# Two transformer-like blocks on one core: the first block's dense products made 512 wide, its gates moved to transposed heads, its differential heads put into fixed TensorE steps

## The chip, the cores and the metric

The kernel runs on one core of one Trainium2 chip. It computes two different blocks one after the other for a sequence of 512 positions and a model width of 1024, in float32 accuracy. The metric is the device time of the whole kernel in microseconds (us); lower is better. The engines are named as in the profile: PE (TensorE, matmul), PEld (its weight loads), DVE (VectorE), ACT (ScalarE), POOL (GpSimd), SP (SyncE, which issues the DMAs).

## The reference

The change is in the first block alone. Cut to what matters, it is:

```python
h = rms_norm(x, norm_g)                                # x: 512 x 1024
z = h @ w_in                                           # 9216 columns, split into ten parts:
q_r, k_r, v_r, gate_r, q_d, k_d, v_d, gate_d, mg_r, mg_d = split(z)
o_r = rms_norm(retention(q_r, k_r, v_r))               # 8 heads, 4 chunks of 128, state carried from chunk to chunk
y_r = (o_r * silu(gate_r)) @ ret_w_o
qd, kd = rms_norm(q_d), rms_norm(k_d)                  # 8 heads, two 64-wide halves each
p = softmax(qd kd^T - slope * dist)                    # causal, one for each half
o_d = rms_norm((p[0] - lam * p[1]) @ v_d)              # differential attention
y_d = (o_d * silu(gate_d)) @ diff_w_o
m = sigmoid(mg_r) * y_r + sigmoid(mg_d) * y_d
x = x + m @ w_out
```

The second block (`..._2`) is another attention layer on that `x`; it is about a third of the span, and its code stays as it is but for the names of some buffers.

## The kernel before

**Products.** Every dense product is made of three matmuls on split operands (`mm3`, L314 to L317): each float32 operand is held as a rounded `hi` and a remainder `lo`, and `hi*hi + hi*lo + lo*hi` is summed in PSUM. Weights come through a `Streamer` in a fixed order (`st.add`, `st.get`): a part of 512 KB is loaded by SP into `wr` (2 buffers), ACT rounds it to `wh` (L128), DVE subtracts to `wl` (L130); `wh` and `wl` have 4 buffers each.

**Two forms of dense product.** `dense_T` has 128 weight columns stationary and all 512 positions moving: its output is transposed (columns on partitions), 512 wide. `dense_TM` has 128 positions stationary and a weight of 256 columns moving: its output has positions on partitions, two tiles of 256 columns share a PSUM tile, and all of one position tile's eight k steps come before the next tile's. `v_r`, `g_r`, `q_d`, `k_d`, `v_d`, `g_d` go through `dense_TM` (tile `dps`), four weights of 256 columns each; `q_r`, `k_r` (`rps`), `mg_*` and `y_*` (`mps`) go through `dense_T`. The output projection `wo` is a `dense_TM` of its own (tile `ops` with `mh`, `ml`).

**Heads.** A pair of retention heads is one chain over four chunks (`rsp`, `rop`, `stp`, `sbd`). A differential head has four steps t of 128 queries: two pairs of score matmuls (`sp`), DVE adds the table `tb` and takes the minimum (L479), ACT exponentiates (L483), DVE joins the two halves (L671 to L673), PE transposes (`apt`), ACT copies (`aT`), PE multiplies with the values (`dop`); at the end the row norm (POOL, L259 and L260), `gated` (L454) multiplies with norm and gate, and `to_oT` transposes (`ogp`) and splits the result.

**Order.** Up to the last weight of `wo` no order of PE is written down: a planner with simulated times takes from the program, instruction by instruction, what it thinks is ready, earlier lines first, and fixes each engine's order when the kernel is built. The program's own order is: retention by groups with its gates, `q_d0 k_d0 v_d0 g_d0`, `mg_r` and `y_r`, then head pair by head pair the attention and the next pair's dense products, `mg_d`, `y_d`, `wo`. From `wo3` on, through the second block, PE runs in the program's order (`tc.manual_schedule`), where one attention step, a share of dense work (`fill`), and the transposes and products of earlier steps follow each other. PSUM: `ps_d` 3 buffers (dense), `ps_t` 2, `ps_s` 2, `ps_o` 1.

Of the kernel before, what the change touches and what calls it, by code (L numbers as in the profile page):

```python
# [32 lines left out]
T_AT = [(0, 2), (0, 5), (1, 0), (1, 2), (1, 4), (1, 6)]  # L33
# [10 lines left out]
QK_BUFS = 12  # L44
LAM0 = 0.8 - 0.6 * math.exp(-0.0)
# [101 lines left out]
def two_block_kernel(ctx: ExitStack, tc: tile.TileContext, A: dict, out: bass.AP):  # L147
# [31 lines left out]
    for g in range(2):  # L179
        for hp in (2 * g, 2 * g + 1):  # L180
            add_k8(f"v_r{hp}", w_in, 1024 + 256 * hp)
            add_k8(f"g_r{hp}", w_in, 2048 + 256 * hp)
            if hp == 2 * g:
                add_k8(f"q_r{g}", w_in, 256 * g)
                add_k8(f"k_r{g}", w_in, 512 + 256 * g)

    def add_diff(hp):
        for nm, base in (("q_d", 3072), ("k_d", 4096), ("v_d", 5120), ("g_d", 6144)):
            add_k8(f"{nm}{hp}", w_in, base + 256 * hp)

    add_diff(0)
    for g in range(4):
        add_k8(f"mg_r{g}", w_in, 7168 + 256 * g)
        add_k8(f"y_r{g}", ret_w_o, 256 * g)
    for hp in range(1, 4):
        add_diff(hp)
    for g in range(4):
        add_k8(f"mg_d{g}", w_in, 8192 + 256 * g)
    for g in range(4):
        add_k8(f"y_d{g}", diff_w_o, 256 * g)  # L200
    for g in range(4):
        add_k8(f"wo{g}", w_out, 256 * g)
# [44 lines left out]

    def spread_row(row, pool):
        ones = pool.tile([1, P], F32, name="ones")
        nc.vector.memset(ones, 1.0)  # L250
        full = pool.tile([P, D], F32, name="full")
        for i in range(2):
            ps = ps_s.tile([P, S], F32, name="rowp", tag="s")
            nc.tensor.matmul(ps, ones, row[:, S * i : S * i + S], start=True, stop=True)
            nc.scalar.activation(full[:, S * i : S * i + S], ps, AF.Copy)
        return full
# [62 lines left out]
    def dense_T(tiles, n0, act_hi, act_lo, name):  # L319
        ps = ps_d.tile([P, S], F32, name=name, tag="d")  # L320
        for kt in range(KT):
            hi, lo = tiles[kt // 4]
            k4 = kt % 4
            mm3(ps, hi[:, k4, n0 : n0 + P], lo[:, k4, n0 : n0 + P],
                act_hi[kt], act_lo[kt], kt == 0, kt == KT - 1)
        return ps

    def dense_TM(tiles, tp, act_hi, act_lo, name, n=256):
        ps = ps_d.tile([P, 2, n], F32, name=name, tag="d")
        for i in range(2):  # L330
# [54 lines left out]
    oT_pool = ctx.enter_context(tc.tile_pool(name="oT", bufs=8))  # L385
# [6 lines left out]
    def new_oT(name):  # L392
        hi = oT_pool.tile([P, S], F32R, name=name + "h", tag="oh")
        lo = oT_pool.tile([P, S], F32R, name=name + "l", tag="ol")
        return hi, lo
# [56 lines left out]
    def gated(o4, scal, w4, og4):  # L452
        for i in range(4):
            nc.vector.scalar_tensor_tensor(og4[:, i, :], o4[:, i, :], scal[:, i : i + 1], w4[:, i, :],  # L454
                                           op0=ALU.mult, op1=ALU.mult)

    def to_oT(og, h, col, name):
        pt = ps_t.tile([P, NT, P], F32, name="ogp", tag="t")
        for t in range(NT):
            nc.tensor.transpose(pt[:, t, :], og[:, t, h * P : (h + 1) * P], ident)  # L460
# [730 lines left out]
```

## Time and profile before

| | us |
|---|---|
| three runs | 972.47, 975.05, 977.28; median 975.05 |
| the profiled execution, its own time | 973.76 |
| its span from first to last instruction | 971.7 |
| mean granted TensorE clock | 0.982 of full |

The profile page gives busy time by engine, the span in slices, and the chain of work that ended last. Matmul ends are modelled and matmuls overlap, so the summed or mean time of a matmul is longer than the distance from one start to the next; that distance, the pace, is what a stream of matmuls costs. Windows are stretches of the span in us.

### The profile page before, as it was taken

Reading aid. Unit: us, or ns where it says so; the run is one execution under the profiler, and the core shown is the slowest. Engines: PE = TensorE matmul, PEld = TensorE weight load, DVE = VectorE, ACT = ScalarE, POOL = GpSimd, SP = SyncE. Lnnn points to the kernel's source line nnn. Section 1 sums busy time; section 2 is a strip of 40 time slices with the busy share of each in tenths; the row PEclk is TensorE's granted clock in tenths of the full one; section 3 lists DMA queues with packets and bytes.
Section 4 is the critical chain, followed back from the end, with each engine's and each line's share of the span. In section 5 each row is a group of like instructions: output and inputs, shape, how many; then the busy total and the mean of one; then the engine's idle time right before and its main releaser. Section 6 shows DMA issues by size and latency. Waiting matters only on the chain.

```text
span 971.7 us, 16383 instructions
## 1 busy us (share of the span) xinstructions
PE 940.3 (97%) x6457; PEld 858.0 (88%) x6457; DVE 556.3 (57%) x1255; ACT 439.3 (45%) x917; POOL 208.7 (21%) x242
## 2 busy tenths in 40 slices
PE   7899999999999999999997988999999899999998
PEld 6889989999888999999996876899998778999886
DVE  4544434463332647647655465535556897778884
ACT  5323222343222545555644453233446666666650
POOL 2000001032000016115113100034146563332000
PEclk9999999999999999999998998999999899999999
DMA  6451232135343322212221212544242231211412
GB/s 202 135 170 45 87 109 87 48 118 165 109 131 129 96 79 87 73 60 88 70 77 59 85 48 65 171 136 153 67 136 70 57 97 44 66 44 45 142 55 87
DMA packets 78047, 92.18 MB, mean 95 GB/s; under 512 B 5081, under 2 KB 66409, under 8 KB 77971
## 3 DMA queue, kind: packets, MB, share of 16 engines
q1 hardware_dynamic: 77970, 91.14, 29.9%
q8 instruction: 51, 0.84, 0.3%
q14 instruction: 26, 0.21, 0.1%
HBM read 84.82 MB, written 8.93 MB: 96 GB/s over the span
## 4 chain that ended last, share of the span: by engine, by line
PE 88%; DVE 6%; DMA 2%; ACT 1%; issue 1%; SPq 1%; POOL 1%; ACTq 0%; POOLq 0%; DVEq 0%
PE dps L315 9%; PE dps L317 9%; PE dps L316 9%; PE mps L315 6%; PE mps L316 6%; PE mps L317 6%; PE ops L315 3%; PE ops L316 3%; PE ops L317 3%; PE aps L315 2%; PE aps L316 2%; PE aps L317 2%; PE dop L681 2%; PE rps L315 1%; PE rps L317 1%; PE rps L316 1%
## 5 line engine op out<-in xcount | busy, mean ns | idle before, releaser
L316 PE MATMUL dps<-wl,h1h 128*128 128x256 f32 x768 | 221.2, 288 | 3.4 <-DVE wl L130 3.4
L315 PE MATMUL dps<-wh,h1h 128*128 128x256 f32 x768 | 222.6, 290 | 1.3 <-ACT h1h L277 1.3
L317 PE MATMUL dps<-wh,h1l 128*128 128x256 f32 x768 | 221.6, 289 | 0.2 <-DVE h1l L278 0.2
L130 DVE TENSOR_TENSOR wl<-wr,wh 128x1024 fp32r<-128x1024 f32 (+2 forms) x115 | 141.4, 1231 | 127.6 <-ACT wh L128 124.9
L128 ACT ACTIVATE wh<-wr 128x1024 fp32r<-128x1024 f32 (+1 forms) x132 | 137.4, 1042 | 166.6 <-PE mps L316 60.0
L316 PEld LDWEIGHTS dps<-wl,h1h 128*128 128x128 f32 x768 | 147.6, 192 | 4.2 <-DVE wl L130 3.8
L315 PEld LDWEIGHTS dps<-wh,h1h 128*128 128x128 f32 x768 | 147.6, 192 | 3.6 <-ACT h1h L277 1.8
L317 PEld LDWEIGHTS dps<-wh,h1l 128*128 128x128 f32 x768 | 147.5, 192 | 1.4 <-issue 0.5
L315 PE MATMUL aps<-wh,h2h 128*128 128x256 f32 x192 | 57.0, 297 | 0.0
L316 PE MATMUL aps<-wl,h2h 128*128 128x256 f32 x192 | 54.3, 283 | 0.0
L317 PE MATMUL aps<-wh,h2l 128*128 128x256 f32 x192 | 54.3, 283 | 0.0
L663 POOL TENSOR_SCALAR tb<-dist 128x512 f32<-128x512 f32 x8 | 13.7, 1712 | 186.2 <-DVE nm L479 156.6
L315 PE MATMUL mps<-h1h,wh 128*128 128x512 f32 x128 | 51.3, 401 | 0.9 <-ACT td L721 0.9
L317 PE MATMUL mps<-h1h,wl 128*128 128x512 f32 x128 | 51.1, 399 | 0.0
L316 PE MATMUL mps<-h1l,wh 128*128 128x512 f32 x128 | 50.8, 397 | 0.0
L483 ACT ACTIVATE p<-sc,nm 128x128 f32<-128x128 f32 (+3 forms) x64 | 35.7, 559 | 33.0 <-DVE nm L479 29.4
L130 POOL TENSOR_TENSOR wl<-wr,wh 128x1024 fp32r<-128x1024 f32 (+2 forms) x17 | 38.1, 2242 | 40.9 <-ACT wh L128 31.6
L1009 ACT ACTIVATE p<-p,nm 128x128 f32<-128x128 f32 (+1 forms) x64 | 35.7, 558 | 20.3 <-DVE nm L1006 19.9
L479 DVE CUSTOM_DVE_ANT_0 sc<-sp,tb 128x128 f32<-128x128 f32 (+3 forms) x64 | 30.3, 488 | 25.4 <-PE sp L312 25.0
L260 POOL TENSOR_TENSOR gnrs<-gnrs,mhalf 128x8 f32<-128x8 f32 x24 | 40.4, 1687 | 1.8
L316 PEld LDWEIGHTS aps<-wl,h2h 128*128 128x128 f32 x192 | 36.7, 191 | 0.3
L317 PE MATMUL ops<-wh,ml 128*128 128x256 f32 x128 | 36.9, 290 | 0.0
(297 smaller groups left out, 2379.5 us busy)
## 6 DMA issues: line engine op xcount, KB each, us to landing
wr<-in_w_in_dram SPq DMA_DIRECT2D x92, 512.0 KB, 3.6
wr<-in_w_out_dram SPq DMA_DIRECT2D x16, 512.0 KB, 3.5
wr<-in_ret_w_o_dram SPq DMA_DIRECT2D x8, 512.0 KB, 3.6
wr<-in_diff_w_o_dram SPq DMA_DIRECT2D x8, 512.0 KB, 3.2
rep_dram<-rev_dram SPq DMA_DIRECT2D x8, 320.0 KB, 8.8
m_dram<-mth SPq DMA_DIRECT2D x8, 256.0 KB, 2.5
mr<-m_dram SPq DMA_DIRECT2D x8, 256.0 KB
x<-in_x_dram SPq DMA_DIRECT2D x4, 512.0 KB
```

Source lines behind the costliest of these rows:

```text
L128: nc.scalar.activation(hi, raw, AF.Copy)
L130: eng.tensor_tensor(lo, raw, hi.bitcast(F32), op=ALU.subtract)
L260: nc.gpsimd.tensor_tensor(dst, dst, mhalf[:, :n], op=ALU.pow)
L315: nc.tensor.matmul(ps, lh, rh, start=start, stop=False)
L316: nc.tensor.matmul(ps, lh, rl, start=False, stop=False)
L317: nc.tensor.matmul(ps, ll, rh, start=False, stop=stop)
L479: nc.vector.tensor_tensor_reduce(sc[:, :n], sp[:, :n], table[:, S - n : S], scale=-1.0, scalar=3.0e38, op0=ALU.add, op1=ALU.min, accum_out=nm)
L483: nc.scalar.activation(p[:, :n], sc[:, :n], AF.Exp, scale=-1.0, bias=nm, accum_out=den)
L663: nc.gpsimd.tensor_scalar(tb, dist, -(2.0 ** -(head + 1)), None, op0=ALU.mult)
L681: nc.tensor.matmul(o_ps[:, t, :], aT[:, kt, :], r["v"][:, kt, h * P : (h + 1) * P], start=kt == 0, stop=kt == t)
L1009: nc.scalar.activation(p[:, :n], p[:, :n], AF.Exp, scale=-1.0, bias=nm, accum_out=den)
```

## The change

**Widths.** `v_r`, `q_d`, `k_d`, `v_d` and `wo` become two weights of 512 columns instead of four of 256, loaded in four parts of 256 rows (`add_wide`). The new `dense_TM` holds two PSUM tiles (two position tiles) and walks k once for both. `g_r` and `g_d` go through `dense_T`.

**Gates.** The heads' outputs are only scaled by their norm, transposed (`to_oT`, one ACT copy with the gain) and kept as `oraw`; `gate_oT` then applies the gate on the transposed head and splits. `y_r` is evicted by ACT and stored to `y_dram`; `mg_r` comes later, loads it back, multiplies and stores to `m_dram`.

**Order.** Retention: `v_r0`, all of `q_r k_r`, two chains, `v_r1`, two chains; then `g_r0 g_r1 q_d0 k_d0 v_d0 g_r2 g_r3`. From there PE runs in the program's order: 32 steps (head, t), with transposes one step and value products two steps behind (`D_LAG`), and dense products handed out between them at a rate written in `D_RUNS` (steps from, to, weights). `y_d` walks k once for two tiles. The norm gain of the second block is loaded as a broadcast instead of being spread by PE (`spread_row`, tile `rowp`). `oT` buffers become one ring of 16; `T_AT` places the transposes of the second block's first tiles later.

```diff
-T_AT = [(0, 2), (0, 5), (1, 0), (1, 2), (1, 4), (1, 6)]
+T_AT = [(0, 2), (0, 5), (1, 3), (1, 6), (2, 3), (2, 6)]
+
+
+D_LAG = 1
+D_RUNS = ((0.0, 6.5, ("y_r0", "y_r1", "y_r2", "y_r3")),
+          (6.5, 10.0, ("mg_r0", "mg_r1")),
+          (10.0, 13.3, ("q_d1", "k_d1")),
+          (13.3, 17.0, ("v_d1",)),
+          (17.0, 36.0, ("g_d0", "g_d1", "mg_r2", "mg_r3", "mg_d0", "mg_d1", "g_d2", "mg_d2", "mg_d3", "g_d3")))
...
+    def add_wide(key, w, c0):
+        parts = []
+        for quarter in range(4):
+            src = w[256 * quarter : 256 * quarter + 256, c0 : c0 + 512]
+            parts.append((src.rearrange("(k p) n -> p k n", p=P), 2, 512))
+        st.add(key, parts)
+    for key in (("v_r0", "q_r0", "k_r0", "q_r1", "k_r1", "v_r1", "g_r0", "g_r1", "q_d0", "k_d0", "v_d0",
+                 "g_r2", "g_r3") + sum((r[2] for r in D_RUNS), ()) + ("y_d0", "y_d1", "y_d2", "y_d3", "wo0", "wo1")):
...
+    def dense_T(tiles, i, act_hi, act_lo, done):
+        ps = ps_d.tile([P, S], F32, name="dps", tag="d")
+        n = slice(P * i, P * i + P)
         for kt in range(KT):
             hi, lo = tiles[kt // 4]
-            k4 = kt % 4
-            mm3(ps, hi[:, k4, n0 : n0 + P], lo[:, k4, n0 : n0 + P],
-                act_hi[kt], act_lo[kt], kt == 0, kt == KT - 1)
-        return ps
-
-    def dense_TM(tiles, tp, act_hi, act_lo, name, n=256):
-        ps = ps_d.tile([P, 2, n], F32, name=name, tag="d")
-        for i in range(2):
-            c = slice((2 * tp + i) * P, (2 * tp + i + 1) * P)
+            mm3(ps, hi[:, kt % 4, n], lo[:, kt % 4, n], act_hi[kt], act_lo[kt], kt == 0, kt == KT - 1)
+            if kt == KT - 1:
+                done(i, ps)
+            yield 3 * S
+
+    def dense_TM(tiles, act_hi, act_lo, done, at=None):
+        for tp in range(2):
+            ps = [ps_d.tile([P, S], F32, name="tps", tag="d") for _ in range(2)]
             for kt in range(KT):
-                hi, lo = tiles[kt // 4]
-                k4 = kt % 4
-                mm3(ps[:, i, :], act_hi[:, kt, c], act_lo[:, kt, c],
-                    hi[:, k4, :n], lo[:, k4, :n], kt == 0, kt == KT - 1)
-        return ps
+                hi, lo = tiles[kt // 2]
+                if at is not None:
+                    at(tp, kt)
+                for i in range(2):
+                    c = slice((2 * tp + i) * P, (2 * tp + i + 1) * P)
+                    mm3(ps[i], act_hi[:, kt, c], act_lo[:, kt, c], hi[:, kt % 2, :], lo[:, kt % 2, :],
+                        kt == 0, kt == KT - 1)
+                    if kt == KT - 1:
+                        done(2 * tp + i, ps[i])
+                    yield 3 * S
...
-    oT_pool = ctx.enter_context(tc.tile_pool(name="oT", bufs=8))
+    oT_pool = ctx.enter_context(tc.tile_pool(name="oT", bufs=16))
...
+        raw = oT_pool.tile([P, S], F32, name="oraw", tag="o")
+        nc.scalar.activation(raw, flat(pt), AF.Copy, scale=col)
+        return raw
+
+    def gate_oT(ps, raw, pool):
+        th = pool.tile([P, S], F32, name="gth", tag="th")
+        nc.scalar.activation(th, ps, AF.Tanh, scale=0.5)
+        nc.vector.scalar_tensor_tensor(th, th, 1.0, ps, op0=ALU.add, op1=ALU.mult)
+        nc.vector.tensor_tensor(th, th, raw, op=ALU.mult)
+        hi, lo = new_oT("og")
+        split(hi, lo, th)
...
+                for h in range(2):
+                    nc.vector.tensor_tensor(og[h][:, 2 * cp : 2 * cp + 2, :], o_ps[:, :, h, :],
+                                            rs[:, h : 4 : 2, None].to_broadcast([P, 2, P]), op=ALU.mult)
...
+        vr[0], gen = values("v_r0")
+        run(gen)
         for g in range(2):
+            decayed("q_r", g)
+            decayed("k_r", g)
+        retain(0)
+        retain(1)
+        vr[1], gen = values("v_r1")
+        run(gen)
+        retain(2)
+        retain(3)
...
+        def diff_qk(key):
+            qn = wp.tile([P, NT, 512], F32, name="dqn", tag="tm")
+
+            def done(tt, ps):
+                group_norm(ps.rearrange("p (g w) -> p g w", w=64), qn[:, tt, :].rearrange("p (g w) -> p g w", w=64),
+                           8, 64, 1.0 / 64, wp)
+
+            yield from dense_TM(st.get(key), hhi, hlo, done)
+            qkd[key] = qn
...
+        def diff_prep(nm, head):
+            pt = ps_t.tile([P, NT, P], F32, name="dpt", tag="t")
+            for tt in range(NT):
+                nc.tensor.transpose(pt[:, tt, :], qkd[f"{nm}_d{head // 4}"][:, tt, head % 4 * P : head % 4 * P + P], ident)
+            if nm == "q":
+                qk[head] = [stack_q(wp, flat(pt), gcol[:, 16:17])]
+            else:
+                qk[head].append(stack_k(wp, flat(pt)))
...
+        def diff_scores(head, t):
...
+            for j in range(2):
+                sp = ps_s.tile([P, S], F32, name="sp", tag="s")
+                mm2(sp, qk[head][0][j], qk[head][1][j], cq, n)
+                p = wp.tile([P, S], F32, name="p", tag="p", bufs=P_BUFS)
+                nm = stat.tile([P, 1], F32, name="nm", tag="nm")
+                nc.vector.tensor_tensor_reduce(p[:, :n], sp[:, :n], tables[head][:, S - n : S], scale=-1.0,
+                                               scalar=3.0e38, op0=ALU.add, op1=ALU.min, accum_out=nm)
+                den = stat.tile([P, 1], F32, name="den", tag="den")
+                nc.scalar.activation(p[:, :n], p[:, :n], AF.Exp, scale=-1.0, bias=nm, accum_out=den)
...
+                og = wp.tile([P, NT, P], F32, name="og", tag="og")
+                nc.vector.tensor_tensor(og, o_ps, rs[:, :, None].to_broadcast([P, NT, P]), op=ALU.mult)
+                og_of[head] = og
+        def project_r(key):
+            g = int(key[-1])
+            tl = st.get(key)
+
+            def done(i, ps):
+                y = wp.tile([P, S], F32, name="my", tag="m")
+                nc.scalar.activation(y, ps, AF.Copy)
+                nc.sync.dma_start(y_dram[2 * g + i], y)
...
+        for key in ("g_r0", "g_r1", "q_d0", "k_d0", "v_d0"):
+            run(makers[key[:-1]](key))
+        diff_prep("q", 0)
+        diff_prep("k", 0)
+        for key in ("g_r2", "g_r3"):
+            run(makers[key[:-1]](key))
+
+        pe_order = ExitStack()
+        pe_order.enter_context(tc.manual_schedule(engines={mybir.EngineType.PE}))
...
+        def fill_d(at):
+            while runs:
+                a, b, gens, spent, total = runs[0]
+                due = total * (at - a) / (b - a) if at < b else float("inf")
...
+        steps = [(head, t) for head in range(8) for t in range(NT)]
+        p_of, aT_of = {}, {}
+        for i in range(len(steps) + D_LAG + 3):
+            if i < len(steps):
+                head, t = steps[i]
+                p_of[i] = diff_scores(head, t)
+                if t in (1, 2) and head < 7:
+                    diff_prep("qk"[t - 1], head + 1)
+            fill_d(i + 0.5)
+            if 0 <= i - D_LAG < len(steps):
+                aT_of[i - D_LAG] = diff_T(p_of.pop(i - D_LAG), steps[i - D_LAG][1])
+            fill_d(i + 1.0)
+            k = i - D_LAG - 1
+            if 0 <= k < len(steps):
+                diff_weigh(*steps[k], aT_of.pop(k))
+            k -= 1
+            if 0 <= k < len(steps) and steps[k][1] == NT - 1:
+                head = steps[k][0]
+                o_raw["d", head] = to_oT(og_of.pop(head), gcol[:, 8 + head : 9 + head])
+        fill_d(1e9)
...
+            ps2 = [ps_d.tile([P, S], F32, name="yps", tag="d") for _ in range(2)]
+            for kt in range(KT):
+                hi, lo = tl[kt // 4]
+                for i in range(2):
+                    n = slice(P * i, P * i + P)
+                    mm3(ps2[i], hi[:, kt % 4, n], lo[:, kt % 4, n], odT[kt][0], odT[kt][1], kt == 0, kt == KT - 1)
+            for i in range(2):
+                done(i, ps2[i])
...
-        row = xp.tile([1, D], F32, name="row2")
-        nc.sync.dma_start(row, A["norm_gain_2"][0:1, :])
-        g2 = spread_row(row, xp)
+        g2 = xp.tile([P, D], F32, name="g2")
+        bcast_row(g2, A["norm_gain_2"][0:1, :], D)
...
+            def at(tp, kt):
+                if g == 1 and tp == 1 and kt == T0_AT:
+                    to_hT(xg[0], 0, hhi, hlo)
```

## Rows read from the trace of the kernel before

**Rows 1.** From the page: busy time, share of the span and instructions of each engine; then the chain that ended last, by engine.

```profile
PE 940.3 (97%) x6457; PEld 858.0 (88%) x6457; DVE 556.3 (57%) x1255; ACT 439.3 (45%) x917; POOL 208.7 (21%) x242
PE 88%; DVE 6%; DMA 2%; ACT 1%; issue 1%; SPq 1%; POOL 1%; ACTq 0%; POOLq 0%; DVEq 0%
```

**Rows 2.** Windows: stretch, its length, busy us (and instructions) of PE, PEld, DVE, ACT and POOL, granted TensorE clock, DMA share, GB/s.

```profile
0.00:30.00 30.00, 21.78 (x119) 18.57 (x120) 14.89 (x23) 13.54 (x23) 6.83 (x17) 0.94 0.65 204
30.00:515.00 485.00, 485.00 (x3443) 454.54 (x3442) 238.93 (x491) 194.41 (x363) 73.13 (x82) 1.00 0.31 98
330.00:515.00 185.00, 185.00 (x1473) 181.00 (x1472) 109.28 (x266) 99.68 (x233) 46.39 (x48) 1.00 0.24 76
515.00:595.00 80.00, 68.18 (x321) 55.01 (x320) 40.87 (x105) 36.92 (x88) 16.64 (x22) 0.91 0.15 46
715.00:800.00 85.00, 78.61 (x522) 68.92 (x521) 67.73 (x188) 52.10 (x119) 49.81 (x52) 0.95 0.28 77
800.00:960.00 160.00, 159.85 (x1234) 143.48 (x1234) 124.50 (x330) 96.22 (x222) 36.73 (x34) 0.99 0.19 60
```

**Rows 3.** Groups of PE by line and shape over the span: the 256-wide products of the first block (one of the three matmuls of `mm3`; the other two have as many). Columns: line, engine, operation, out<-in, shape, count | busy us, mean ns | idle before.

```profile
L315 PE MATMUL dps<-wh,h1h 128*128 128x256 f32 x768 | 222.6, 290 | 1.3 <-ACT h1h L277 1.3
...
L317 PE MATMUL ops<-wh,ml 128*128 128x256 f32 x128 | 36.9, 290 | 0.0
```

**Rows 4.** PE in order of time (start us, modelled us, what), the first and last row of three unbroken streams: 36 matmuls of 256 columns (positions stationary), 19 of 512 (weights stationary), and 14 of 512 (positions stationary, second block's last projection).

```profile
639.77 0.28 PE L315 MATMUL ops<-wh,mh 128*128 128x256 f32 x1
...
643.97 0.28 PE L317 MATMUL ops<-wh,ml 128*128 128x256 f32 x1
...
599.70 0.39 PE L316 MATMUL mps<-odl,wh 128*128 128x512 f32 x1
...
603.78 0.39 PE L316 MATMUL mps<-odl,wh 128*128 128x512 f32 x1
...
964.72 0.39 PE L316 MATMUL ops<-wl,mixh 128*128 128x512 f32 x1
...
967.66 0.39 PE L317 MATMUL ops<-wh,mixl 128*128 128x512 f32 x1
```

**Rows 5.** The window 515 to 595 once more, for the instructions of one tile each, in this order: `mps`, `sp`, `dop`, `apt`, `dpt`, `ogp`. The first column after the length is PE, with the count in brackets; the others are the engines that touch the tile.

```profile
515.00:595.00 80.00, 51.89 (x193) 37.61 (x193) 0.00 (x0) 4.47 (x8) 0.91 0.15 46
515.00:595.00 80.00, 7.27 (x32) 5.40 (x32) 7.42 (x16) 0.91 0.15 46
515.00:595.00 80.00, 7.17 (x48) 6.60 (x47) 3.38 (x12) 4.06 (x18) 0.91 0.15 46
515.00:595.00 80.00, 4.06 (x20) 2.72 (x20) 0.00 (x0) 3.44 (x8) 0.91 0.15 46
515.00:595.00 80.00, 3.35 (x16) 2.20 (x16) 5.75 (x8) 5.10 (x8) 0.91 0.15 46
515.00:595.00 80.00, 3.20 (x12) 1.84 (x12) 2.24 (x3) 2.05 (x3) 0.91 0.15 46
```

**Rows 6.** The chain that ended last, two pieces of it (start us, us, what, count): the pace of transposes and of the value products.

```profile
338.70 0.44 PE apt L677 x4
...
342.49 0.89 PE dop L681 x8
```

**Rows 7.** PE in order of time, three of the rows with idle time before them in 515 to 595 (in brackets: idle us and who ended it).

```profile
518.92 1.01 PE L460 MATMUL ogp<-ident,og 128*128 128x128 f32 x4 [2.28 <-DVE og L454]
...
580.46 1.65 PE L315 MATMUL mps<-odh,wh 128*128 128x512 f32 x3 [1.42 <-ACT odh L281]
...
590.55 1.16 PE L460 MATMUL ogp<-ident,og 128*128 128x128 f32 x4 [2.72 <-DVE og L454]
```

**Rows 8.** PE in order of time: the spreading of the norm gain, and the first product of the second block.

```profile
632.19 1.98 PE L254 MATMUL rowp<-row,ones 1*128 1x512 f32 x4
...
675.21 0.45 PE L315 MATMUL cps<-wh,h2h 128*128 128x416 f32 x1 [0.57 <-ACT h2h L277]
```

**Rows 9.** The start, in order of time: the one long wait of PE, and what held the DVE queue ahead of it.

```profile
28.07 0.38 PE L316 MATMUL dps<-wl,h1h 128*128 128x256 f32 x1 [2.97 <-DVE wl L130]
...
26.58 0.29 DVE L444 TENSOR_TENSOR lp<-lv 128x128 f32<-128x128 f32 x1 [4.12 <-DMA lv<-in_diff_lk_dram]
```

**Rows 10.** Groups of DVE, ACT and POOL by line and shape up to 640 us (columns as in Rows 3): weight remainder, score pass, joining of halves, the chain of the q/k norm.

```profile
L130 DVE TENSOR_TENSOR wl<-wr,wh 128x1024 fp32r<-128x1024 f32 x93 | 114.3, 1230 | 112.4 <-ACT wh L128 109.9 <-PE dpt L650 1.5
...
L479 DVE CUSTOM_DVE_ANT_0 sc<-sp,tb 128x512 f32<-128x512 f32 x16 | 11.0, 685 | 5.0 <-PE sp L312 4.7
...
L673 DVE SCALAR_TENSOR_TENSOR p<-p,cf 128x512 f32<-128x512 f32 x8 | 6.0, 752 | 0.4
...
L375 ACT ACTIVATE dqn<-dps 128x512 f32<-128x512 f32 x16 | 9.5, 591 | 16.3 <-PE dps L317 16.2
...
L377 ACT ACTIVATE gnq<-dqn 128x512 f32<-128x512 f32 x16 | 9.5, 624 | 0.7 <-DVE gns L379 0.5 <-DVE rss L573 0.2
...
L379 DVE TENSOR_REDUCE gns<-gnq 128x8 f32<-128x512 f32 x16 | 10.6, 680 | 14.3 <-ACT gnq L377 14.2
...
L260 POOL TENSOR_TENSOR gnrs<-gnrs,mhalf 128x8 f32<-128x8 f32 x16 | 27.3, 1713 | 1.2
L259 POOL TENSOR_SCALAR gnrs<-gns 128x8 f32<-128x8 f32 x16 | 7.2, 451 | 7.8 <-DVE gns L379 6.7
L382 DVE TENSOR_TENSOR dqn<-dqn,gnrs 128x512 f32<-128x512 f32 x16 | 11.0, 690 | 9.4 <-POOL gnrs L260 9.2
L371 ACT ACTIVATE gth<-dps 128x512 f32<-128x512 f32 x16 | 9.5, 596 | 22.3 <-PE dps L317 22.3
```

More of the change, by code (lines that the diff above doesn't have):

```diff
@@ new lines, in diff_T, with diff_weigh @@
+        def diff_T(p, t):
+            pt = ps_t.tile([P, NT, P], F32, name="apt", tag="t")
+            for kt in range(t + 1):
+                nc.tensor.transpose(pt[:, kt, :], p[:, kt * P : (kt + 1) * P], ident)
+            aT = wp.tile([P, NT, P], F32, name="aT", tag="aT")
+            nc.scalar.activation(aT[:, : t + 1, :], pt[:, : t + 1, :], AF.Copy)
+            return aT
+        o_now, og_of = {}, {}
+        def diff_weigh(head, t, aT):
+            if t == 0:
+                o_now[0] = ps_o.tile([P, NT, P], F32, name="dop", tag="o")
+            o_ps = o_now[0]
+            hc = slice(head % 4 * P, head % 4 * P + P)
+            for kt in range(t + 1):
+                nc.tensor.matmul(o_ps[:, t, :], aT[:, kt, :], vd[head // 4][:, kt, hc], start=kt == 0, stop=kt == t)
+            r0, ss = heads[head]
+            sq = wp.tile([P, P], F32, name="dsq", tag="sq")
+            nc.scalar.activation(sq, o_ps[:, t, :], AF.Square, scale=r0[:, t : t + 1], accum_out=ss[:, t : t + 1])
+            if t == NT - 1:
@@ new lines, in two_block_kernel, with merge_d, done @@
+        tds = {}
+        def merge_d(key):
+            g = int(key[-1])
+            tl = st.get(key)
+            def done(i, ps):
+                n = 2 * g + i
+                if n % 4 == 0:
+                    tds["now"] = wp.tile([P, 4, S], F32, name="td", tag=("vv", "tm")[n // 4])
+                tds[n] = tds["now"][:, n % 4, :]
+                nc.scalar.activation(tds[n], ps, AF.Tanh, scale=0.5)
+            for i in range(2):
+                yield from dense_T(tl, i, hh, hl, done)
@@ new lines, in two_block_kernel @@
+        makers = {"y_r": project_r, "mg_r": merge_r, "q_d": diff_qk, "k_d": diff_qk, "v_d": diff_v,
+                  "g_r": lambda key: gates(key, orT),
+                  "g_d": lambda key: gates(key, odT), "mg_d": merge_d}
+        dense_cost = {"q_d": 64 * 3 * S // 2, "k_d": 64 * 3 * S // 2, "v_d": 64 * 3 * S // 2}
+        for key in ("g_r0", "g_r1", "q_d0", "k_d0", "v_d0"):
[4 more added lines that the diff above has]
+            run(makers[key[:-1]](key))
@@ new lines, in two_block_kernel @@
+        pe_order = ExitStack()
+        pe_order.enter_context(tc.manual_schedule(engines={mybir.EngineType.PE}))
+        runs = [[a, b, [(makers[k[:-1]], k) for k in keys], 0,
+                 sum(dense_cost.get(k[:-1], 16 * 3 * S) for k in keys)] for a, b, keys in D_RUNS]
+        def fill_d(at):
+            while runs:
+                a, b, gens, spent, total = runs[0]
+                due = total * (at - a) / (b - a) if at < b else float("inf")
+                while gens and spent < due:
+                    if isinstance(gens[0], tuple):
+                        gens[0] = gens[0][0](gens[0][1])
+                    n = next(gens[0], None)
+                    if n is None:
+                        gens.pop(0)
+                    else:
+                        spent += n
+                runs[0][3] = spent
+                if gens:
+                    return
+                runs.pop(0)
@@ L725, in two_block_kernel, with done @@
             tl = st.get(f"y_d{g}")
-            for i in range(2):
+            def done(i, ps):
                 n = 2 * g + i
@@ L1092, in mixed @@
             yield from long
-        def run(gen):
-            for _ in gen:
-                pass
         aqn, v_a = {}, {}
```

399 lines of the change are left out of this document (146 added, 253 removed).

## The prediction

> **What bounds the kernel now.** I read the page first [rows 1]: PE is busy 97% of the span, its work is 88% of the chain that ended last, and no other engine passes 57%. A busy PE is not yet a PE at its pace, so the second view is the windows [rows 2]: from 30 to 515 us PE has no idle time at all and the full clock. There only less PE work can help; what DVE, ACT or POOL do is worth nothing. The exceptions are the start (8.2 us idle of 30, clock 0.94), 515 to 595 (11.8 us idle of 80, clock 0.91) and 715 to 800 (6.4 us idle of 85, clock 0.95). The third is in the second block, whose code stays.
>
> The third view is the order of time, for the pace, since modelled ends mislead: the mean of a 256-wide matmul is 290 ns [rows 3], and two of those against one 512-wide would promise far too much. In an unbroken stream 36 matmuls of 256 columns start in 4.20 us, 35 distances of 120.0 ns; 19 of 512 columns start in 4.08 us, 18 distances of 226.7 ns; and 14 of 512 with positions stationary, the geometry of the new products, take 2.94 us, 13 distances of 226.2 ns [rows 4]. So a pair of 256-wide costs 240.0 ns, one 512-wide 226.7: widening is worth 13.3 ns a pair, not a factor.
>
> **The change part by part. Widths.** The group `dps` has 768 matmuls for each of its three lines, 2304 in all [rows 3]: 2304 x 0.1200 = 276.5 us. After it, half as many of 512: 1152 x 0.2267 = 261.2. That is 15.3 us less. `wo` (`ops` with `m`, 3 x 128 [rows 3]) goes from 384 x 0.1200 = 46.1 to 192 x 0.2267 = 43.5: 2.6 us less. Since PE has no idle time there, all of it comes off the end, as long as the weights come in time: the bytes are the same, and a 512 KB part now feeds PE as long as before (24 wide matmuls, 5.4 us, for one subtract of 1.23 us [rows 10]).
>
> Here a rule speaks against the change. The Trainium skill, page "TensorE: Matmul & The Clock Gate", section "Back-to-back issue gap", gives a warm gap of N/2.4 + 2.5 ns; worked out from it, as an estimate, a pair of 256 costs 218 ns and one 512 costs 216, so that 1344 pairs would save 3 us, not 17.9. The trace does not agree on the 256-wide form: 120.0 ns where the rule gives 109. The row decides, and the rule stays as a rival.
>
> **The end of attention.** In 515 to 595 the work in PE's pace is: 193 `mps` x 0.2267 = 43.8; 32 `sp` of 128 to 512 columns, 320 on average, between the two paces at some 0.147, 4.7; 48 `dop` x 0.111 = 5.3; 48 transposes (20 + 16 + 12) x 0.11 = 5.3 [rows 5, 6]. Together 59.0 of 80 us: 21.0 us are lost, as idle time and as half clock after it. The waits show why [rows 7]: the last head pairs' chains (row norm, gate, transposes, split) are all that is left, PE waits for `og` (2.28, 2.72) and the first `y_d` waits for the last split head (1.42). After the change ten dense weights are spread over steps 17 to 36, so each head's chain has a product beside it; the last gate needs only tanh 0.60 [rows 10] and three DVE or ACT passes of about 0.7 after its product, some 3 us, while `y_d0` with k outermost has seven k steps x 2 x 3 x 0.2267 = 9.5 us before it wants the last head. I take the 21.0 us as gone. The cover is those products; without it the same wait returns (a rival).
>
> **Small ones.** The spreading of the gain, 1.98 us of PE [rows 8], goes; its replacement is one more 512 KB load, first used after 10.9 us of `wo` matmuls. Behind the transposes of the second block's first tile stand two k steps of two tiles, 12 x 0.2267 = 2.7 us, where six 256-wide matmuls stood, 0.7 us; that covers the wait of 0.57 [rows 8]. Gates: per pair of heads eight small `gated` passes and two gain splits become scalings, two products and two splits, about the same DVE time, and ACT gains some 15 us over the whole block; both are hidden by PE in a stretch with DVE at 49% and ACT at 40% [rows 2]. 16 more DMAs of 256 KB on SP: hidden, DMA share 0.31 there [rows 2]. Retention's chains keep the planner's order, and it has more dense work at hand (`v_r1`, `g_r0`, `g_r1`) than the chains last: nothing. If that cover failed, each of four chains could cost some us; I keep it for the range. Sum of gains: 15.3 + 2.6 + 21.0 + 2.0 + 0.6 = 41.5 us.
>
> **What it adds.** (a) Start: the first weight now has four parts, and PE can open only three position tiles (`ps_d`), so before the fourth part it has 54 matmuls, 12.2 us; it had 13.2 us of work before the wait of 2.97 us, whose cause stays (DVE's queue stood 4.12 us on the `lambda` load, ahead of a subtract [rows 9]). +1 us; bounds -3.0 (the wait gone) and +5.4 (one part's worth). (b) Keys of heads 4 to 7: `k_d1` ends in step 13 and its transposes stand in step 14. Behind its last matmul come copy 0.59, square 0.62, sum 0.68, on POOL 0.45 + 1.71 for each of two tiles, and the multiply 0.69 [rows 10]: about 7 us with the hand-overs. PE has between them 1.2 + 3.0 us of `v_d1`, 0.5 of products and 0.7 of scores: 5.4. PE waits, everything behind it too: +2 us; bounds 0 and 7. (c) The fixed order: PE can't pass a late operand any more. A step is about 8 us (dense 16 x 48 x 0.2267 + 3 x 96 x 0.2267 = 239 us, attention from [rows 5] 15.3 / 2 = 7.7 us a head, 61 in all: 300 us over 36 steps), and a transpose comes one and a half steps of products after its scores, 10 us, against a chain of two score passes 1.5, exp 0.9, joining 1.2 [rows 10], about 4.5 us with hand-overs. DVE's load by [rows 10]: a head has eight score passes of at most 0.69, four joinings of at most 0.75, four query and key splits of about 0.7, one scaling and some ten small ones, 13 us at most; the dense part has 44 subtracts of 1.23, eight norm tiles of 1.37, eight gates of three passes of 0.7 and six merges, 87 us: 190 of 300, or 64%. It lies between 330 to 515 (59%, planner's order, no loss) and 800 to 960 (78%, fixed order, 0.15 us idle, clock 0.99) [rows 2]; the bound above is 715 to 800 (80%, fixed order): 7.5% idle and 5% of the clock, 12%, which would be 36 us. I take 1%, 3 us, by the nearer rows. (d) `y_d` takes two PSUM tiles of three: each change of weight waits for an eviction of 0.7 us behind 1.4 us of cover: +0.5; bounds 0 and 4. Sum 6.5 us.
>
> Net: 41.5 - 6.5 = 35.0 us. On the profiled execution's 973.76 that is 938.8; the median of the runs is 1.3 us higher, 975.05, which gives 940.
>
> **The rivals.** *The tail only moves.* The fixed steps lose in waits about what the end of attention loses now: 975.05 - 20.5 + 1 = 956. For it: the same chains, and PE can't reorder; against: 10 us of cover for 4.5. *Slower:* the fixed order turns DVE's queue into PE's. DVE works in its own order; a score pass behind one or two subtracts of 1.23 us keeps `sp` (two buffers) and the next transposes waiting, PE stands, its clock falls. It decides from a loss of 41.5 - 3.5 = 38 us on, 1.2 us in each of 32 steps; at 1.5 us a step it is 48 us, 985 in all. For it: 715 to 800 loses 12% in just this way, which at 300 us is 36 and would give 973, no change; against: 64% DVE instead of 80%. *The width gives nothing:* if wide matmuls in these streams come at 240 ns, as two 256-wide do, 17.9 us stay: 958. By the page's rule above it would be 955, as an estimate. Against: the 226.2 ns of the same geometry [rows 4]. *Better:* start and keys lose nothing and the fixed order is clean: 931.
>
> **How the numbers follow.** Forecast 0.72, the tail moves 0.13, no gain of width 0.04, fixed order as in 715 to 800 (no change) 0.03, worse than that 0.04, better 0.04. The likeliest's own range is 932 to 948. The range to report must leave out no more than two in ten: 930 to 957 holds the forecast, the moved tail and part of the better case. A change of 0.5% (4.9 us) is about what a measurement here can tell from none: faster 0.72 + 0.13 + 0.04 + 0.04 = 0.93, same 0.03, slower 0.04.
>
> **What would show it.** In the profile after: 1152 matmuls of 512 columns where `dps` had 2304, pace 227 ns, no 256-wide ones in the first block; PE without idle time at the last heads, clock 1.00 there; no wait of `ogp` for `og`; at the start a wait for `wl` of the fourth part of about 3 us; one wait of `dpt` for `dqn` of 2 us near step 14; `y_d` starts without waiting for the last head. Wrong would be: idle time of PE at `apt` or `sp` in many steps, ended by DVE; waits in the retention chains; or a pace above 235 ns.

## The result, and the profile after

The changed kernel takes 950.85 us (median of four runs, 948.72 to 952.61) against 974.64 for the kernel before on the same chip: a ratio of 0.9754, 95% interval 0.9719 to 0.9788. That is 24 us less, where 35 were forecast. Its profiled execution has a span of 950.1 us at a mean granted clock of 0.992, against 971.7 at 0.982.

The page's busy time and chain of the changed kernel, which answer [rows 1]:

```profile
PE 919.7 (97%) x5109; PEld 778.6 (82%) x5109; DVE 556.8 (59%) x1222; ACT 451.5 (48%) x923; POOL 206.9 (22%) x234
PE 84%; DVE 6%; ACT 3%; DMA 3%; POOL 2%; issue 1%; SPq 0%; ACTq 0%; POOLq 0%; DVEq 0%
```

PE is still the bound, with 1,348 instructions fewer. The windows that answer [rows 2] (stretch, length, busy us and instructions of PE, PEld, DVE, ACT and POOL, granted clock, DMA share, GB/s):

```profile
0.00:30.00 30.00, 24.86 (x104) 18.49 (x105) 15.61 (x25) 14.93 (x25) 6.83 (x17) 1.00 0.70 215
30.00:130.00 100.00, 99.31 (x472) 81.55 (x471) 42.36 (x79) 30.82 (x38) 5.43 (x6) 1.00 0.38 112
130.00:225.00 95.00, 89.18 (x420) 70.09 (x420) 39.46 (x69) 30.71 (x46) 19.36 (x25) 0.96 0.23 70
225.00:505.00 280.00, 278.26 (x1397) 234.00 (x1396) 170.20 (x366) 155.13 (x331) 63.55 (x70) 1.00 0.36 112
505.00:600.00 95.00, 95.00 (x450) 79.25 (x450) 48.70 (x83) 38.71 (x72) 2.60 (x4) 1.00 0.33 105
600.00:640.00 40.00, 37.79 (x160) 30.73 (x159) 13.12 (x17) 9.21 (x15) 6.14 (x4) 0.96 0.42 140
640.00:690.00 50.00, 46.63 (x276) 43.06 (x275) 27.03 (x58) 21.04 (x52) 14.60 (x22) 0.97 0.40 123
```

The 12 us of idle time at the end of the attention are gone: 505 to 600, where the last heads and `y_d` now lie, has none, at the full clock. In exchange there is idle time from 130 to 225, where the kernel before had none at all, and more of it from 600 to 690.

Idle time alone hides the half clock that follows a wait, so I made a second measure, used below: PE's *loss* in a stretch is the sum, over its instructions, of the distance from one start to the next less the pace of that kind (227 ns for 512 columns, 120 for 256, 109 to 111 for a transpose or a value product, as in [rows 4, 6]). It is worked out from the whole trace. Before and after it is, in us (the kernel before is cut at the same places of the program: 605, 665 and 715 us where the others have about 600, 645 and 700; the second row of the changed kernel is another execution of it):

```
                0-40  40-130  130-225  225-380  380-505  attention's  wo    first    second   all
                                                         end, y_d           product  block
before          13.6   0.6      1.7      0.3      0.6      22.5       2.6    1.2     19.9     63.0
after           10.4   2.1     14.6      1.7      3.9       0.5       4.1    5.7     16.8     59.7
after, again    12.0   1.6     15.2      1.7      3.8       0.6       3.8    5.7     16.6     61.1
```

But for the start, the two executions of the changed kernel differ by at most 0.6 us in a stretch. The level hangs on the paces taken: with the median distance of each kind over all traces a value moves by up to 3.2 us, a difference between two kernels by up to 1.4.

The span fell by 21.6 and the loss by 3.3, so PE's work fell by 18.3 us. The reading is plain: the work that was to go went, the 22 us at the end of the attention went too, and about as much came back elsewhere, 13 of it in one stretch.

That stretch, PE's two long waits in it (start us, us, what, in brackets the idle us and who ended it):

```profile
177.38 0.57 PE L307 MATMUL tps<-wh,h1h 128*128 128x512 f32 x1 [2.07 <-ACT dqn L376]
218.14 0.44 PE L655 MATMUL dpt<-ident,dqn 128*128 128x128 f32 x2 [1.63 <-DVE rv L589]
```

Ahead of the first, ACT in order of time: the eviction `dqn` that PE needs stands behind two conversions of the next weight, and these wait for its DMA.

```profile
173.32 1.06 ACT L137 ACTIVATE wh<-wr 128x1024 fp32r<-128x1024 f32 x1 [3.52 <-DMA wr<-in_w_in_dram]
174.29 0.58 ACT L547 ACTIVATE rsq<-rop 128x512 f32<-128x512 f32 x1
175.79 1.06 ACT L137 ACTIVATE wh<-wr 128x1024 fp32r<-128x1024 f32 x1 [0.92 <-DMA wr<-in_w_in_dram]
176.75 0.58 ACT L376 ACTIVATE dqn<-tps 128x512 f32<-128x512 f32 x1
```

After a wait the clock falls: behind the one at 177 us eight 512-wide matmuls start some 427 ns apart, nearly twice the pace, and the window just there has a granted clock of 0.61, so mostly the lower level, 1.2 GHz. A wait of 2 us thus costs nearly 4.

```profile
177.00:180.00 3.00, 2.62 (x7) 2.06 (x8) 2.23 (x4) 0.33 (x1) 1.12 (x2) 0.61 0.61 180
```

The other two new waits, in the output product and in the first product of the second block:

```profile
616.90 0.50 PE L307 MATMUL tps<-wh,mh 128*128 128x512 f32 x1 [2.21 <-DVE x L865]
671.91 0.43 PE L307 MATMUL cps<-wh,h2h 128*128 128x416 f32 x1 [2.64 <-DVE rab L906]
```

### The profile page after: what moved, and what is told of

Read it like the earlier page. It is cut to its first block, busy times and chain, and to the rows that moved or that the text cites. A ratio compares the mean times of both kernels' runs of the same rounds, so it can differ in the third digit from the quotient of the medians.

```text
span 950.1 us, 13694 instructions
## 1 busy us (share of the span) xinstructions
PE 919.7 (97%) x5109; PEld 778.6 (82%) x5109; DVE 556.8 (59%) x1222; ACT 451.5 (48%) x923; POOL 206.9 (22%) x234
## 4 chain that ended last, share of the span: by engine, by line
PE 84%; DVE 6%; ACT 3%; DMA 3%; POOL 2%; issue 1%; SPq 0%; ACTq 0%; POOLq 0%; DVEq 0%
PE dps L307 9%; PE dps L309 9%; PE dps L308 9%; PE tps L307 7%; PE tps L309 6%; PE tps L308 6%; PE aps L307 2%; PE aps L308 2%; PE aps L309 2%; DMA wr<-in_w_in_dram 2%; PE dop L707 2%; PE ops L307 2%; PE ppt L1114 2%; PE yps L308 2%; PE yps L307 2%; PE ops L308 2%
## 5 line engine op out<-in xcount | busy, mean ns | idle before, releaser
L307 PE MATMUL dps<-h1h,wh 128*128 128x512 f32 x320 | 128.2, 401 | 0.0
L309 PE MATMUL dps<-h1h,wl 128*128 128x512 f32 x320 | 125.3, 392 | 0.0
L308 PE MATMUL dps<-h1l,wh 128*128 128x512 f32 x320 | 125.0, 390 | 0.0
L307 PE MATMUL tps<-wh,h1h 128*128 128x512 f32 x256 | 104.0, 407 | 4.7 <-ACT dqn L376 2.5
L309 PE MATMUL tps<-wh,h1l 128*128 128x512 f32 x256 | 102.8, 401 | 0.1
L308 PE MATMUL tps<-wl,h1h 128*128 128x512 f32 x256 | 101.8, 398 | 0.8 <-DVE wl L139 0.8
L309 PEld LDWEIGHTS dps<-h1h,wl 128*128 128x128 f32 x320 | 60.1, 188 | 13.1
L307 PEld LDWEIGHTS dps<-h1h,wh 128*128 128x128 f32 x320 | 60.1, 188 | 11.8
L308 PEld LDWEIGHTS dps<-h1l,wh 128*128 128x128 f32 x320 | 60.2, 188 | 11.5
L307 PEld LDWEIGHTS tps<-wh,h1h 128*128 128x128 f32 x256 | 49.0, 191 | 16.9 <-ACT dqn L376 4.5
```

The source lines that it names most:

```text
L307: nc.tensor.matmul(ps, lh, rh, start=start, stop=False)
L308: nc.tensor.matmul(ps, lh, rl, start=False, stop=False)
L309: nc.tensor.matmul(ps, ll, rh, start=False, stop=stop)
```

## The experiments

Each is an edit of the changed kernel. The ratios are to the kernel before, with the 95% interval. The intervals of most single edits overlap with that of the changed kernel, so gains of 1 to 3 us are read from the loss of a stretch and not from the time. The changed kernel itself, run again beside the first four:

> The changed kernel again, beside the others of this call: all theories expect its recorded time, about 951 us, 24 us under the kernel before.

It took 951.64 us, ratio 0.9755 (0.9731 to 0.9779).

### What is the width worth?

```diff
+    def mm3_half(ps, lh, ll, rh, rl, start, stop):
+        for f in (0, 256):
+            m = slice(f, f + 256)
+            nc.tensor.matmul(ps[:, m], lh, rh[:, m], start=start and f == 0, stop=False, skip_group_check=True)
...
-                    mm3(ps[i], act_hi[:, kt, c], act_lo[:, kt, c], hi[:, kt % 2, :], lo[:, kt % 2, :],
+                    mm3_half(ps[i], act_hi[:, kt, c], act_lo[:, kt, c], hi[:, kt % 2, :], lo[:, kt % 2, :],
```

> Every product that the change made 512 wide is run as two 256-wide halves; the order and everything else stay. Theory (the width is worth what its rows say): 1,344 matmuls of 512 columns become 2,688 of 256, each pair 13.3 ns longer (2 x 120.0 less 226.7), so +17.9 us on the changed kernel, about 969 us. Rival (the width buys nothing, the whole gain is from the order): within 3 us of the changed kernel.

958.62 us, ratio 0.9834 (0.9813 to 0.9854): 7 us slower, between the two. The loss tells why: it fell from 61.1 to 47.7 while the span rose by 4.0 in the profiled executions, so the work rose by 17.4 us, and the theory's 17.9 are nearly there. But 13.4 us of loss went at the same time, 8 of them from 130 to 225 (15.2 to 7.3); the wait at 177 isn't in this trace. Both had a part right: the width is worth what its pace says, and in this kernel more than half of that is lost again in waits that the split kernel doesn't have. Whether the width brings them, or the order that the planner makes around it, this run can't separate.

The rule that was weighed against it (the Trainium skill, page "TensorE: Matmul & The Clock Gate", section "Back-to-back issue gap") would give 3 us for this edit, as an estimate from its isolated gap; the 17.4 us of work decide against it. In the changed kernel 192 products `dps` run unbroken, of which the first and the last start here, 191 distances of 226.7 ns:

```profile
40.43 0.39 PE L307 MATMUL dps<-h1h,wh 128*128 128x512 f32 x1
...
83.73 0.39 PE L309 MATMUL dps<-h1h,wl 128*128 128x512 f32 x1
```

### What took the stall at the end of the attention away?

Three candidates: the order written by hand, the dense products spread between the steps, and `y_d` with both blocks in step.

The order given back to the planner up to the last `wo` weight:

```diff
-        pe_order.enter_context(tc.manual_schedule(engines={mybir.EngineType.PE}))
...
+            if g:
+                pe_order.enter_context(tc.manual_schedule(engines={mybir.EngineType.PE}))
```

> The order of TensorE written by hand begins only at the output product, as in the kernel before; in the differential part the planner is free to place the dense products, which stand spread in the program as in the changed kernel. Theory (the fixed order is what took the stall away): 10 to 20 us slower than the changed kernel, with TensorE idle again at the end of the attention. Rival (that the products stand spread in the program is enough): within 3 us.

946.22 us, ratio 0.9705 (0.9689 to 0.9722). My theory fell: without the fixed order the kernel is 5 us *faster*, and the end of the attention loses 0.4 us. From 505 to 605 PE has no idle time:

```profile
505.00:605.00 100.00, 100.00 (x472) 83.39 (x472) 51.41 (x84) 40.27 (x73) 2.60 (x4) 1.00 0.32 106
```

What the planner wins back are the wait for `dpt` at 399 us (loss of 380 to 505 down from 3.8 to 2.1) and the one in `wo` (3.8 to 0).

Nine of the ten weights ahead of the last five steps, in the fixed order:

```diff
-          (17.0, 36.0, ("g_d0", "g_d1", "mg_r2", "mg_r3", "mg_d0", "mg_d1", "g_d2", "mg_d2", "mg_d3", "g_d3")))
+          (17.0, 31.0, ("g_d0", "g_d1", "mg_r2", "mg_r3", "mg_d0", "mg_d1", "g_d2", "mg_d2", "mg_d3")),
+          (31.0, 36.0, ("g_d3",)))
```

> The fixed order stays, but the dense products that stood in its last five steps (about 17.8 us of TensorE work) run ahead of them, all but the last weight. Theory (it is the dense work between the chain's steps that covers the chain): the waits on the differential chain return in those steps, 5 to 15 us slower than the changed kernel. Rival (the chain needs no cover once its order is fixed): within 2 us.

952.98 us, ratio 0.9778 (0.9760 to 0.9797): 1.3 us slower, within the rival's 2 and less than the theory's 5, with a loss of 2.4 us in place of 0.6. One weight was still left behind the last heads, so the cover was thinned and not gone. The next run takes that away too; the gate's product is ready early, and only its multiply and split follow the last transposes:

```diff
+          (17.0, 31.0, ("g_d0", "g_d1", "mg_r2", "mg_r3", "mg_d0", "mg_d1", "mg_d2", "mg_d3", "g_d2", "g_d3")))
...
+                th = gate_th(ps, wp)
+                if key == "g_d3":
+                    late[6 + i] = th
+                else:
+                    out[2 * g + i] = gate_oT(th, o_raw.pop((kind, 2 * g + i)))
```

> The fixed order stays, but all ten dense weights run ahead of the last five steps, the gate of the last two heads too: its tanh is kept, and only the multiply and the split follow the last transposes. So the last steps hold nothing but the attention's own work. Theory (one gate weight, 10.9 us of products, left behind the last heads is cover enough, which is why the earlier experiment with nine weights ahead lost little): now the waits at the end of the attention come back, 8 to 20 us slower than the changed kernel. Rival (the chain has become short enough without the gate in it to need no cover, the last gate included): within 3 us of it.

965.40 us, ratio 0.9906 (0.9880 to 0.9931): 12.4 us slower than the kernel with one weight left. The stall is back, 13.1 us of loss in place of 2.4, with a wait for `og` as in [rows 7] and a longer one for the joined scores `p`, and a clock of 0.77 where it lies:

```profile
545.00:575.00 30.00, 22.56 (x101) 18.94 (x100) 13.10 (x29) 12.29 (x30) 2.40 (x4) 0.77 0.16 50
560.39 1.08 PE L701 MATMUL apt<-ident,p 128*128 128x128 f32 x4 [3.83 <-DVE p L695]
568.45 1.09 PE L456 MATMUL ogp<-ident,og 128*128 128x128 f32 x4 [3.01 <-DVE og L723]
```

(Of the rest some 3 us lie in the second block, of which more below.) Then `y_d` block by block:

```diff
-            ps2 = [ps_d.tile([P, S], F32, name="yps", tag="d") for _ in range(2)]
-            for kt in range(KT):
...
+            for i in range(2):
+                run(dense_T(tl, i, [t[0] for t in odT], [t[1] for t in odT], done))
```

> The output product of the differential heads is run block by block, as in the kernel before, and not with both blocks in step behind each head; the rest is the changed kernel. Theory (the cover comes from the gate product, and the last head is split before it is wanted): within 2 us of the changed kernel. Rival (the two blocks in step, 9.5 us before they want the last head, are what took the stall away): 4 to 10 us slower, with a wait for the last heads at their first product.

953.66 us, ratio 0.9783 (0.9757 to 0.9810), 2.0 us slower, and the end of the attention loses 0.7 us, as in the changed kernel; the second block alone loses some 3 us more (below). The rival falls. So what took the stall away is dense work that is left when the last heads' chains run, and one weight of 10.9 us is nearly enough. In the changed kernel the last scores stand at 527 us, and products that need only `h` go on to 559:

```profile
527.22 0.39 PE L304 MATMUL sp<-ksl,qst 128*128 128x512 f32 x1
559.22 0.39 PE L309 MATMUL dps<-h1h,wl 128*128 128x512 f32 x1
```

In the kernel before the last product on `h` stands at 556 us and the last scores at 576:

```profile
556.12 0.39 PE L317 MATMUL mps<-h1h,wl 128*128 128x512 f32 x1
576.15 0.40 PE L312 MATMUL sp<-ksl,qst 128*128 128x512 f32 x1
```

There the gate was an input of the head's last step, so `g_d` had to come first. But the 192 products of `mg_d` need no head either; they stood behind the heads in the program, and the planner used them up earlier. So it isn't shown that the cover needs the gate on transposed heads: the old gates, with an order that keeps `mg_d` back, weren't tried. Nor was the planner without a fixed order and with nine weights placed early.

### Where did the new waits come from?

Four edits of one cause each. The gathered values `rv` out of the ring that holds the retention's values:

```diff
-        rv = wp.tile([8, 640], F32, name="rv", tag="vv")
         for i in range(2):
+            rv = wp.tile([8, 320], F32, name="rv", tag="m")
```

> The gathered values rv leave the ring of buffers that they share with the retention's values and take two halves of another ring. Theory (the wait of 1.63 us for rv at 218 us and the half clock behind it come from that ring): 3 to 4 us faster than the changed kernel, and the wait gone. Rival (the wait is for something else, or another follows at once): within 1 us.

953.31 us, ratio 0.9770 (0.9748 to 0.9791): no gain. Yet the wait is gone, and 130 to 225 loses 9.7 us in place of 15.2. A full ring wasn't what held `rv` in the changed kernel, though: PE's last read of the retention's values starts at 207.44 us, and DVE writes `rv` at 217.61 and 218.61, the first time behind a `dqn` that waited 0.93 us for POOL. In this run it writes `rv` later still, at 222.19 and 223.79, with the transposes `dpt` behind that. So the edit moved these instructions in the planner's order; why it did isn't shown.

The gain went again: 1.9 us to a wait at 261 us for a gated head, and 4.0 in the second block (20.6 in place of 16.6). There the code is the same, and PE's order is fixed by hand; the order of DVE isn't. PE's waits at that place, in the changed kernel and in this one:

```profile
732.52 0.52 PE L1114 MATMUL ppt<-ident,p 128*128 128x128 f32 x3 [1.63 <-DVE rd L1107]
736.87 0.66 PE L1114 MATMUL ppt<-ident,p 128*128 128x128 f32 x4 [0.67 <-DVE pTl L270]
740.18 0.63 PE L1054 MATMUL apt<-ident,aqn 128*128 128x128 f32 x4 [1.01 <-DVE qst L285]
```

```profile
735.81 0.66 PE L1054 MATMUL apt<-ident,aqn 128*128 128x128 f32 x4 [2.56 <-DVE pTl L270]
738.91 0.47 PE L1114 MATMUL ppt<-ident,p 128*128 128x128 f32 x1 [1.46 <-DVE qst L285]
```

I compared the order in which DVE gets its instructions in the second block, over all kernels of this study; one or two weight splits at its start are left out. The loss there goes by it without an exception:

```
DVE's order in the second block             loss of the second block, us
as in the changed kernel: after, planner,   16.6 to 16.8
  early, g2 later, mixed, four edits
as in the kernel before: before, rv,        19.3 to 20.6
  transposes at old places, narrow q_d0
two others: split; no cover; y_d by block   19.2 to 19.8
```

PE's and POOL's orders are the same in all of them; ACT's differs in the same groups as DVE's. So 3 to 4 us of the second block go with what the planner makes of edits hundreds of us ahead of it. Which of the two orders costs them isn't shown, as no run changes one alone; "DVE's order" below stands for both.

The broadcast of the gain behind the first two loads of `x`:

```diff
-        bcast_row(g2, A["norm_gain_2"][0:1, :], D)
...
+            if tt == 1:
+                bcast_row(g2, A["norm_gain_2"][0:1, :], D)
```

> The broadcast load of the 512 KB gain of the second block is issued behind the first two loads of x for the residual, not ahead of them. Theory (the residual add at 615 us waited for x behind that load): the wait of 2.21 us and about 1 us of half clock go, 2 to 3 us faster than the changed kernel. Rival (the load was hidden or another wait takes its place): within 1 us.

947.27 us, ratio 0.9726 (0.9702 to 0.9749), and the add that waited 8.75 us for the DMA of `x` now waits for PE, as it should. The two rows, of the changed kernel and of this one:

```profile
616.15 0.69 DVE L865 SCALAR_TENSOR_TENSOR x<-tps,x 128x512 f32<-128x512 f32 x1 [8.75 <-DMA x<-in_x_dram]
```

```profile
613.16 0.69 DVE L866 SCALAR_TENSOR_TENSOR x<-tps,x 128x512 f32<-128x512 f32 x1 [6.62 <-PE tps L309]
```

The loss in `wo` falls from 3.8 to 1.6; what is left is above all a wait of PE of 0.99 us at 626.10, for a later add that stands behind a weight's subtract on DVE. By the loss that is the 2 to 3 us of the theory.

The transposes at their old places:

```diff
-T_AT = [(0, 2), (0, 5), (1, 3), (1, 6), (2, 3), (2, 6)]
+T_AT = [(0, 2), (0, 5), (1, 0), (1, 2), (1, 4), (1, 6)]
```

> The transposes of the second block's input go back to the six places that they had in the kernel before. Theory (their later places hold the work buffers that the squares of the next stage need): the wait of 2.64 us at 669 us and the half clock behind it shrink, 3 to 4 us faster than the changed kernel. Rival (the earlier transposes meet waits of their own): within 1 us or slower.

948.88 us, ratio 0.9726 (0.9702 to 0.9749). The first product's loss falls from 5.7 to 1.2 us, the theory's gain. In both traces the squares of the next stage begin on ACT right behind the copy of the last transposes, at 668.67 us in the changed kernel and at 663.75 here. 640 to 690 has the full clock:

```profile
640.00:690.00 50.00, 49.27 (x316) 46.25 (x315) 30.17 (x63) 23.56 (x57) 14.79 (x24) 1.00 0.45 137
```

Of that 3.1 us go again with DVE's order in the second block.

Narrow weights between the wide ones:

```diff
-        for key in ("g_r0", "g_r1", "q_d0", "k_d0", "v_d0"):
+        for key in ("g_r0", "q_d0", "g_r1", "k_d0", "g_r2", "v_d0"):
...
-        for key in ("g_r2", "g_r3"):
+        for key in ("g_r3",):
```

> Ahead of the fixed order the narrow gate and key weights stand between the wide ones in the program, so that no wide weight follows another. Theory (the wait of 2.07 us at 177 us is a wide weight that is loaded late and queues an eviction behind its conversion): that wait and the half clock behind it go, 3 to 4 us faster than the changed kernel. Rival (the planner makes the same kind of wait elsewhere): within 1 us.

952.95 us, ratio 0.9774 (0.9755 to 0.9794), no gain. The rival was right: the wait at 177 goes, and in its place come two others, with a loss of 17.5 from 130 to 225:

```profile
214.18 1.12 PE L456 MATMUL ogp<-ident,og 128*128 128x128 f32 x4 [3.84 <-DVE og L553]
221.51 0.47 PE L655 MATMUL dpt<-ident,dqn 128*128 128x128 f32 x1 [2.71 <-DVE dqn L383]
```

So the wide weight was tried alone, with only `q_d0` narrow:

```diff
+        if key == "q_d0":
+            for j in range(2):
+                add_k8(f"qn{j}", w_in, 3072 + 256 * j)
```

> The query weight of the first four differential heads is taken as two 256-wide weights of two parts each, as in the kernel before, and not as one 512-wide weight whose four parts all stay in use until its last position tiles; the rest is the changed kernel. Price of the width: 96 pairs of matmuls by 13.3 ns, 1.3 us. Theory (the four parts, held to the end, delay the next weight's, and the eviction queues behind them): the wait of 2.0 us at 177 us and the half clock behind it, 4 us in all, go, and TensorE's loss from 130 to 225 us falls from 15 to about 11. Rival (the planner's order of the stretch makes the loss, wide or narrow): the loss there stays at 13 or more, with a wait in another place. The order of VectorE in the second block becomes the one that cost 3 us in two of the single runs, so the whole time is read with that taken off: theory 951 to 952, rival 955 or more.

950.62 us, ratio 0.9744 (0.9717 to 0.9771). The stretch loses 10.7 us, near the theory's 11, and the wait at 177 shrinks to 0.75; but the wait for `rv` is gone too, and a new one stands there, for the next wide weight:

```profile
215.94 0.80 PE L311 MATMUL tps<-wl,h1h 128*128 128x512 f32 x1 [2.78 <-DVE wl L139]
```

That the late wide weight makes such waits is thus supported; that it alone makes the loss isn't, since the planner's order of the stretch moves with each edit. Some 5 us of small waits in the retention chains there I can't put down to one cause.

### Four edits together

The diffs of the planner, of `rv`, of the broadcast and of the transposes, on one kernel:

> Four edits on the changed kernel that each took a wait away: the planner free in the differential part, the gathered values out of the ring of the retention's values, the gain's broadcast behind the first loads of x, the transposes at their old places. Each stretch's loss is counted once, by the single runs: 2 to 4 us at 399 and 615 us, about 5 at 216, 4.5 at 669. The order that the planner gives VectorE in the second block is that of the changed kernel here, not the one that took 3 to 4 us back in two of the single runs. Theory (the gains add): 13 to 15 us under the changed kernel, 937 to 939 us. Rival (waits take each other's place): 943 or more.

939.05 us (936.82 to 940.05), ratio 0.9627 (0.9602 to 0.9653): 12 us under the changed kernel, the fastest here and at the upper end of the theory's 937 to 939. The loss is 44.5 us against 61.1: 9.2 from 130 to 225, 1.3 in `wo`, none in the first product, 16.7 in the second block. The gains add once DVE's order in the second block is held in view.

```profile
600.00:640.00 40.00, 40.00 (x182) 33.18 (x182) 14.79 (x19) 11.14 (x19) 9.39 (x10) 1.00 0.52 174
640.00:690.00 50.00, 49.27 (x353) 47.96 (x352) 30.07 (x64) 25.15 (x60) 15.00 (x21) 1.00 0.39 118
```

## Why the prediction was right, and where it was not

- *Widths and `rowp`, 15.3 + 2.6 + 2.0 = 19.9 us of work:* right. The work fell by 18.3, and the split gave 17.4 back where 17.9 were priced.
- *The end of the attention, 21.0 us:* right in size (the loss fell by 22.0) and in mechanism: cover, which without the last product fails. The reasons beside it were not needed: neither the fixed order nor `y_d` in step has a part in it. One row was misread: the wait of 1.42 us was not the first `y_d` waiting for the last head. `y_d` had begun at 556.35 us with the first six heads, at 580.46 it waited for the seventh, and the last came with the wait of 2.72.
- *"As long as weights come in time":* failed. The term compared the time that a part feeds PE with the conversion; it didn't ask how long the parts stay in use. At 177 us an eviction stood behind conversions that waited for a DMA.
- *Retention, "nothing":* the step that failed by most. I reasoned on more dense work at hand, and the stretch 130 to 225 lost 13 us more. Neither long wait there is for a retention chain: one is for the eviction `dqn`, about 4 us with its half clock, one for `rv`, and 5.5 us went when `rv` was moved. The range's "four chains" had the stretch right and not the cause.
- *The load of the gain, "first used after 10.9 us":* wrong question. The gain came in time; `x`, queued behind it, did not. 2 us.
- *The first product of the second block, a gain of 0.6:* not there. PE still waits for `h2h`, 0.46 us at 652.18 where it waited 0.57. *`T_AT`:* not priced at all. The later places put the squares of the next stage back to 668.67 us, and 4.5 us were lost.
- *Start, +1 us:* instead 1.5 to 3 us less. *Keys of heads 4 to 7, +2:* right, a wait of 1.8 us, about 3 with the half clock. *Fixed order, +3:* beyond the keys' wait the planner's order wins nothing there, so near 0. *`y_d`, +0.5:* not seen.
- *The second block, "whose code stays":* its code did, its time didn't; about 3 us less, with DVE's order.

Sum of the loss: -22.0 at the attention's end and -3 each at the start and in the second block, against 12.9 from 130 to 225, 4.7 from 225 to 505, 1.5 from 40 to 130, 1.5 in `wo` and 4.5 in the first product: -3, where the forecast had -21.6 plus 6.5, about -15. The range, whose upper part was the rival of the moved tail, held the time; what moved was not the tail into the fixed steps, but the waits into the stretches around them. The forecast's own range, 932 to 948, missed it; that the reported range held it is in part luck, since its room was left for another reason. (The rival *better* is summed too low: with nothing lost at start, keys and fixed order, 940 less 6 is 934, not 931.)

## What to carry to other kernels

A stall at the end of a chain is cured by work that is left over when the chain runs, and here one weight's worth was nearly enough. Look first for such work that the order uses up too early (here it would be `mg_d`, which wasn't tried), then for an operand, like the gate here, whose use can be moved behind the chain. Price a wider tile twice: by its pace, worth 17.4 us here, and by the waits beside it, of which the split kernel had 13.4 us less; look at what stands in ACT's and DVE's queues behind the conversion of a late weight. Where a planner orders the instructions, compare its order also in the parts that you didn't touch before you put a difference down to your edit.
